# Moving 20 block dots in a hybrid GLA/DSA/PEER decoder kernel: between the gate blocks, a first weight tile fetched early, and a longer spread

## The chip, the cores and the metric

The kernel runs on one core of one Trainium2 chip. The metric is the device time of one launch in microseconds (us); a time in a table is the median of several runs. A profile is one execution of its own, recorded by the hardware profiler, with its own time.

## What is computed

One decoder layer on 512 tokens with model width 1024: two token mixers (gated linear attention and an attention over keys that an indexer selects), merged by sigmoid gates, and then a channel mixer with product keys (PEER). The change lies in the last part, which is, cut to what matters:

```python
q = (h @ w_q).reshape(B, S, PEER_HEADS, PEER_DKEY)
s1, s2 = q[..., :half] @ sub_keys_1.T, q[..., half:] @ sub_keys_2.T
v1, i1 = lax.top_k(s1, 16); v2, i2 = lax.top_k(s2, 16)
best, ci = lax.top_k((v1[..., :, None] + v2[..., None, :]).reshape(B, S, 8, 256), 16)
expert_idx = i1[ci // 16] * 128 + i2[ci % 16]          # 16384 experts
gates = jax.nn.softmax(best, axis=-1)
# per token: 8 heads x 16 experts
u, v = expert_u[expert_idx], expert_v[expert_idx]      # rows of 1024
a = gelu(einsum('td,thkd->thk', h, u)) * gates
out = einsum('thk,thkd->td', a, v)
x = rmsnorm(x + gate2 * out)
```

Everything is float32.

## The kernel before

Tokens come in four tiles of 128. The first two tiles are computed sparsely: GpSimd gathers for each token its expert rows by indirect DMAs (`fetch`), VectorE does the dot products and the weighted sums (`dot`, `add`, in the profile `grow`, `gacc`, `h2n`). This runs as a background generator `gather`, which `pump` moves on a step at a time between the steps of the other work.

The last two tiles (256 tokens) are computed densely, against all 16384 experts in 128 blocks of 128. For each block three things are needed:

- the **dot** (`dots_of(ib)`): the block's rows of `u` (`up`, one 1 MiB load for two blocks) times the 256 tokens, 8 float32 matmuls of 128x256, each of which the trace records as two passes, so 16 rows of `pmm<-h2h,up` on line 184. ScalarE puts the gelu into `kept[:, ib % 48]` (or, for tokens whose gates are there already, into `dg`, and VectorE multiplies `kept` by `dg`, line 956);
- the **gates** of the block: `build_g(Tt)` makes them for 8 tokens a step, 16 steps for a token tile. VectorE makes one-hot matrices `pm` and `eq` (lines 883, 886), ScalarE scales `eq` to `qm`, TensorE multiplies the two for each token (`products`, line 907, 8 matmuls a step, 16 passes), ScalarE copies the product to `gs`; every second step VectorE multiplies the `m` blocks of `kept` that have their dots by the new gates, ScalarE copies the gates of the others up to block 48, and the gates of blocks 48 to 127 go to DRAM (`gd<-gs`);
- the **chunk** `ib` of `dense`: the weights of the block (`kept`, split into a high and a low part `as`) times the block's rows of `v` (`vb`, split into `vs`), 12 matmuls of 128x512 that add into four PSUM banks (`psc`, `ptr`; lines 186 to 188).

The dots of blocks 0 to 47 (`AHEAD`) are made before `dense` starts; `DOTS = (8, 16)` says how many stand in the code ahead of the selection (`pick`) of the first and of the second dense token tile, and the rest follow in a loop with the gate steps of the second tile. While `pick` of the second tile runs, the loop takes two steps of the first tile's gates after each of its parts. The dots of blocks 48 to 127 are spread over the chunks: after chunk `ib`, dots are made up to number 48 + (ib + 1) * 80 // 112. The block's gates are read back as `gtile` (eight blocks in 1 MiB) and multiplied in by `weigh(ib + LEAD)`.

Engines run their instructions in order, and the order is that of a scheduler which moves instructions ahead where tiles allow it, so that the order of the code is only a preference. The tiles of `dense` lie in a pool `dn`, opened after the pool of the routing and of the gates (`rest_eng`) is closed; its addresses become free when that pool's work has ended. Two tiles of the pool `hp`, tags `hh` and `hl`, hold `up` loads of the early dots (the pairs of blocks rotate over two slots `w2`, `hh` and `hl`, so blocks 44 and 45 are in `hh`, 46 and 47 in `hl`), and afterwards `as4` (tag `hh`) and every second `gtile` (tag `hl`). All loads but the gathers stand in one queue, SP's.

Of the kernel before, what the change touches and what calls it, by code (L numbers as in the profile page):

```python
# [9 lines left out]
F32 = mybir.dt.float32  # L10
F32R = mybir.dt.float32r
# [9 lines left out]
P = 128  # L21
T = 512
D = 1024
# [16 lines left out]
NE = 7  # L40
RATE_ADA, RATE_GLA, RATE_DSA, RATE_G, RATE_DENSE = 0.4, 0.75, 0.9, 1.0, 1.05
AHEAD = 48
LEAD = 5
DOTS = (8, 16)
RATE_SEL = 3.0
GB = 16
HG = 4
# [2 lines left out]
NDT = T - TH  # L50
# [9 lines left out]
def hybrid_block_kernel(ctx, tc, x, c_col, w_ada, b_ada, b_col, g1_col, g2_col, wT, wN, wM, w_br, w_o,  # L60
                        w_gu, gla_g, kv_g, w_ukv, w_pq, sk, rows, u_t, v_t, fin_g, out):
    nc = tc.nc
    sb = ctx.enter_context(tc.tile_pool(name="const", bufs=1))
    dr = ctx.enter_context(tc.tile_pool(name="dr", bufs=1, space=DRAM))
    hp = ctx.enter_context(tc.tile_pool(name="acts", bufs=1))
# [45 lines left out]
    def behind(i):  # L111

        pace[0] = i.ins
# [10 lines left out]
    def pmm(narrow=False):  # L124
        turn[2] += 1
        if turn[2] % 3 == 0 and not narrow:
            return pmx()
        return ps.tile([P, 512], F32, name="pmm", bufs=2)
# [16 lines left out]
    def pump(n=1.0):  # L145

        if quiet[0]:
            return
        for b in background:
            b[2] += n * b[1]  # L150
            while b[2] >= 1:
                b[2] -= 1
                next(b[0], None)
# [36 lines left out]
    def projT(dst, src, act):  # L190

        w = [t.rearrange("p (k c) -> p k c", k=KD) for t in (src if isinstance(src, list) else weights(src, D, len(act) == 1))]
        for k in range(KD):
            mm(dst, [t[:, k] for t in w], [t[:, k] for t in act], k == 0, k == KD - 1)
# [18 lines left out]
    def drain(gen):  # L213
        for _ in gen:
            pass
# [660 lines left out]
    def build_g(Tt):  # L876

        TB = 8
        gs = None
        last = ()  # L880
        for t0 in range((Tt - NG) * P, (Tt - NG + 1) * P, TB):
            pm = gb.tile([P, TB, P], F32, name="pm", bufs=2)
            nc.vector.tensor_tensor(pm, iof[:, None, :].to_broadcast([P, TB, P]),
                                    i2T[:, t0:t0 + TB, None].to_broadcast([P, TB, P]), op=ALU.is_equal)
            e = gb.tile([P, TB // 2, P, 2], BF16, name="eq", bufs=2)
            behind(nc.vector.tensor_tensor(
                e, iob[:, None].to_broadcast([P, TB // 2, P, 2]),
                i1T[:, t0:t0 + TB].rearrange("p (g t) -> p g t", t=2)[:, :, None, :].to_broadcast([P, TB // 2, P, 2]),
                op=ALU.is_equal))
            qm = gb.tile([P, TB, P], F32, name="qm", bufs=2)  # L890
            for t in range(TB):
                nc.scalar.activation(qm[:, t], e[:, t // 2, :, t % 2], AF.Copy, scale=gaT[:, t0 + t:t0 + t + 1])
            drain(last)
            if t0 % GB == 0:
                gs = gb.tile([P, P, GB], F32, name="gs", bufs=2)
            last = products(t0, pm, qm, gs)
            pump()
            yield
        drain(last)

    def products(t0, pm, qm, gs):
        b, tb = t0 % GB, t0 // GB
        for t4_ in range(0, 8, 4):
            turn[0] += 1
            p = (psc, ptr)[turn[0] % 2]().rearrange("p (t i) -> p t i", t=4)
            for t in range(4):
                nc.tensor.matmul(p[:, t], pm[:, t4_ + t], qm[:, t4_ + t], start=True, stop=True)
            nc.scalar.copy(gs[:, :, b + t4_:b + t4_ + 4], p.rearrange("p t i -> p i t"))
        if b:

            m, ts_ = made[0], slice(tb * GB, (tb + 1) * GB)
            if m:
                nc.vector.tensor_tensor(kept[:, :m, ts_], kept[:, :m, ts_], gs[:, :m], op=ALU.mult)
            if m < AHEAD:
                nc.scalar.copy(kept[:, m:, ts_], gs[:, m:AHEAD])
            built[0] = (tb + 1) * GB
            nc.sync.dma_start(gd.rearrange("c p b i t -> b p c i t")[tb], gs.rearrange("p (c i) t -> p c i t", i=8)[:, AHEAD // 8:])
        yield
# [16 lines left out]
            nc.vector.scalar_tensor_tensor(y[:, ns], x2[:, ns], r, fing[:, ns], op0=ALU.mult, op1=ALU.mult)  # L935
            nc.sync.dma_start(out[Tt * P:(Tt + 1) * P, ns], y[:, ns])

    up = [None]

    def dots_of(ib):  # L940

        early = dn is None
        if ib % 2 == 0:
            pool, tag, bufs = ((wp, "w2", 2), (wp, "w2", 2), (hp, "hh", 1), (hp, "hl", 1))[ib // 2 % 4] if early else (dn, "up", 2)
            up[0] = pool.tile([P, 2, D], F32, name="up", tag=tag, bufs=bufs)
            nc.sync.dma_start(up[0], u_t[ib // 2])
        p = pmm(True)
        projT(p[:, :NDT], [up[0][:, ib % 2]], h2[1])
        a = kept[:, ib % AHEAD]
        d = built[0] if ib < AHEAD else 0  # L950
        if d < NDT:
            nc.scalar.activation(a[:, d:], p[:, d:NDT], AF.Gelu)
        if d:
            t = gb.tile([P, NDT], F32, name="dg", bufs=2)[:, :d]
            nc.scalar.activation(t, p[:, :d], AF.Gelu)
            behind(nc.vector.tensor_tensor(a[:, :d], a[:, :d], t, op=ALU.mult))
        made[0] += 1

    def dense(first_v):
        banks = [psc, psc, ptr, ptr]  # L960
        acc = [[banks[2 * i + n]() for n in range(2)] for i in range(NT - NG)]
        as4 = hp.tile([P, 4, 2, NDT], F32R, name="as", tag="hh")
        gts = []

        def load_g(c):

            if c < P // 8:
                pool, tag = ((dn, "gtile"), (hp, "hl"))[c % 2]
                gts.append(pool.tile([P, NDT // GB, 8, GB], F32, name="gtile", tag=tag))
                nc.sync.dma_start(gts[-1], gd[c - AHEAD // 8])  # L970

        load_g(AHEAD // 8)

        def weigh(ib):

            if ib < AHEAD:
                return
            if ib % 8 == 0:
                load_g(ib // 8 + 1)
            a3 = kept[:, ib % AHEAD].rearrange("p (b t) -> p b t", t=GB)  # L980
            behind(nc.vector.tensor_tensor(a3, a3, gts[ib // 8 - AHEAD // 8][:, :, ib % 8], op=ALU.mult))

        late_ops = []
        vb = x2 = None
        for ib in range(P):
            if ib < NRAW:
                vc = first_v[ib]
            elif ib % 2 == 0 or ib == NRAW:
                vb = dn.tile([P, 2, D], F32, name="vb", bufs=3)
                nc.sync.dma_start(vb[:, ib % 2:], v_t[ib // 2][:, ib % 2:])  # L990
            if ib >= NRAW:
                vc = vb[:, ib % 2]
            if ib == P - 8:
                x2 = dn.tile([P, NT - NG, D], F32, name="fx", tag="up", bufs=2)
                for i in range(NT - NG):
                    nc.sync.dma_start(x2[:, i], x2d[NG + i])
            if ib + LEAD < P:
                weigh(ib + LEAD)
            a = as4[:, ib % 4]
            v = wp.tile([P, 2, D], F32R, name="vs", tag="w2", bufs=2)  # L1000
            split(a[:, 0], a[:, 1], kept[:, ib % AHEAD])
            split(v[:, 0], v[:, 1], vc)
            a, v = [[t[:, 0], t[:, 1]] for t in (a, v)]
            late_ops.append((ib, a, v))
            stage[0] = ib
            if ib == P - 2:
                continue
            for i in range(NT - NG):
                ts_ = slice(i * P, (i + 1) * P)
                for n in range(2):  # L1010
                    ns = slice(n * 512, (n + 1) * 512)
                    for jb, a, v in late_ops:
                        mm(acc[i][n], [t[:, ts_] for t in a], [t[:, ns] for t in v], jb == 0, jb == P - 1)
            late_ops.clear()
            while made[0] < AHEAD + (ib + 1) * (P - AHEAD) // (P - 16) and made[0] < P:
                dots_of(made[0])
            pump()
        for i in range(NT - NG):
            finish(NG + i, x2[:, i], acc[i])
# [90 lines left out]
    dn = None  # L1110
# [47 lines left out]
    made, built = [0], [0]  # L1158
    building = iter(())
    background[:] = [[gat, RATE_G, 0.0]]  # L1160
    for Tt in range(NG, NT):
        for _ in range(DOTS[Tt - NG]):
            dots_of(made[0])
        for h0 in range(0, 8, HG):
            for _ in pick(Tt, h0):
                next(building, None)
                next(building, None)
                pump(0.6)
        picks_T(Tt)
        drain(building)  # L1170
        building = build_g(Tt)
# [6 lines left out]
    for ib in range(NRAW):  # L1178
        first_v.append(wp.tile([P, D], F32, name="vc", tag="raw", bufs=NRAW))
        nc.sync.dma_start(first_v[ib], v_t[ib // 2][:, ib % 2])  # L1180
    rest_eng.close()
    dn = ctx.enter_context(tc.tile_pool(name="dn", bufs=1, reuse_waits="tile"))
    fing, gate2 = [dn.tile([P, D], F32, name=n) for n in ("fing", "gate2")]
# [72 lines left out]
```

## Time and profile before

| | us |
|---|---|
| median of 3 runs | 1851.52 (1850.68 to 1851.56) |
| the profiled execution | 1843.28 |
| its span, first to last instruction | 1841.6 |
| TensorE (PE) busy in the span | 1717.2 |
| VectorE (DVE) busy | 1430.3 |
| ScalarE (ACT) busy | 718.8 |
| GpSimd (POOL) busy | 555.5 |

The span is the stretch from the first to the last instruction of the profiled execution; its time has 1.7 us around it. An engine's busy time is the sum of its instructions. PE's instructions are pipelined, so that a duration covers the next one's start: the pitch of two starts is what one of them costs when PE is full. The stages meant in this document lie in the span at these places: the dots, the second `pick` and the gates from 957.6 to 1178.2 us, the chunks from 1178.2 to 1829.5, the last normalization from there to 1841.6.

### The profile page before, as it was taken

The numbers are of one execution on the slowest core, as the hardware profiler recorded it, in microseconds if no ns is written. First come the engines' busy times: TensorE is split into PE (matmuls) and PEld (weight loads), VectorE is DVE, ScalarE is ACT, GpSimd is POOL, SyncE is SP. The second block draws the span as 40 slices with busy tenths as digits, with TensorE's granted clock in tenths as the row PEclk, the third lists the DMA queues.
The fourth block names the chain that finished last, engine by engine and source line by source line (L and its number), as shares of the span: only waits on it lengthen the run. The fifth ranks groups of instructions, "written<-read, shape, count | busy, mean of one in ns | idle before, by whom it ended". The sixth has DMA issues, their size and how long they took to land.

```text
span 1841.6 us, 25048 instructions
## 1 busy us (share of the span) xinstructions
PE 1717.2 (93%) x8898; PEld 1461.0 (79%) x8898; DVE 1430.3 (78%) x2985; ACT 718.8 (39%) x1694; POOL 555.5 (30%) x459
## 2 busy tenths in 40 slices
PE   6999999989999988988999889899999999999995
PEld 3887999978767776877778779788888888888874
DVE  5698646438999868766996999388888888788887
ACT  3544465432221124102243878334333333333343
POOL 0013000001454456652432667122222222222220
PEclk9999999989998999989999889999999999999998
DMA  7747556724887799996876999799999999999992
GB/s 289 278 166 281 197 172 212 252 86 178 282 305 250 267 353 375 389 378 239 321 285 248 339 324 382 302 395 407 407 415 398 400 398 414 393 406 405 400 351 116
DMA packets 145567, 573.33 MB, mean 311 GB/s; under 512 B 14481, under 2 KB 41233, under 8 KB 111650
## 3 DMA queue, kind: packets, MB, share of 16 engines
q1 hardware_dynamic: 90146, 303.28, 44.4%
q0 software_dynamic: 55296, 268.46, 37.6%
q8 instruction: 70, 1.15, 0.2%
q14 instruction: 55, 0.45, 0.1%
HBM read 553.86 MB, written 17.83 MB: 310 GB/s over the span
## 4 chain that ended last, share of the span: by engine, by line
PE 40%; issue 22%; DVE 19%; DMA 8%; POOL 8%; ACT 2%; POOLq 0%; SPq 0%; DVEq 0%; ACTq 0%
PE pmm L184 14%; POOL grow L1022 7%; DMA grow<-rows,ids 7%; DVE gacc L1036 3%; DVE grow L1027 3%; PE pmm L187 2%; PE pmm L188 2%; PE pmm L186 2%; PE pmx L184 2%; PE psc L187 1%; PE psc L188 1%; PE psc L186 1%; PE ptr L187 1%; PE ptr L186 1%; PE ptr L188 1%
## 5 line engine op out<-in xcount | busy, mean ns | idle before, releaser
L1022 POOL DMA_INDIRECT grow<-rows,ids x384 | 496.5, 1293 | 842.9 <-DVE h2n L1036 461.1
L184 PE MATMUL pmm<-h2h,up 128*128 128x256 f32 x2048 | 470.7, 383 | 13.4 <-DMA up<-u_t 6.7
L184 PEld LDWEIGHTS pmm<-h2h,up 128*128 128x128 f32 x2048 | 388.3, 192 | 69.6 <-DMA up<-u_t 7.1
L1027 DVE SCALAR_TENSOR_TENSOR grow<-grow,h2n 128x1024 f32<-128x1024 f32 x256 | 310.8, 1220 | 68.3 <-DMA grow<-rows,ids 68.0
L117 DVE TENSOR_TENSOR vs<-vb,vs 128x1024 fp32r<-128x1024 f32 x125 | 152.9, 1223 | 40.5 <-ACT vs L116 40.2
L1036 DVE SCALAR_TENSOR_TENSOR gacc<-grow,dots,gacc 128x1024 f32<-128x1024 f32 x127 | 162.7, 1281 | 15.2 <-DMA grow<-rows,ids 14.8
L1036 DVE SCALAR_TENSOR_TENSOR h2n<-grow,dots,h2n 128x1024 f32<-128x1024 f32 x127 | 162.8, 1282 | 0.0
L116 ACT CAST vs<-vb 128x1024 fp32r<-128x1024 f32 x125 | 130.3, 1043 | 14.0 <-DMA vb<-v_t 10.1
L117 DVE TENSOR_TENSOR w<-raw,w 128x1024 fp32r<-128x1024 f32 x79 | 98.0, 1241 | 46.5 <-ACT w L116 46.2
L186 PE MATMUL psc<-vs,as 128*128 128x512 f32 x256 | 113.9, 451 | 0.0
L187 PE MATMUL psc<-vs,as 128*128 128x512 f32 x256 | 101.8, 398 | 11.2 <-DVE vs L117 11.1
L116 ACT CAST w<-raw 128x1024 fp32r<-128x1024 f32 x79 | 82.7, 1046 | 74.2 <-PE pmm L188 35.6
L1075 ACT ACTIVATE dots<-dots 128x1 f32<-128x1 f32 x128 | 25.8, 202 | 199.1 <-DVE grow L1027 199.0
L116 ACT CAST as<-kept 128x256 fp32r<-128x256 f32 x128 | 51.3, 403 | 128.2 <-PE ptr L187 128.2
L184 PE MATMUL pmm<-hh,raw 128*128 128x256 f32 x416 | 97.6, 382 | 3.6 <-DVE yp L687 1.8
L188 PE MATMUL psc<-vs,as 128*128 128x512 f32 x256 | 100.5, 393 | 0.0
L187 PE MATMUL ptr<-vs,as 128*128 128x512 f32 x256 | 100.1, 391 | 0.0
L188 PE MATMUL ptr<-vs,as 128*128 128x512 f32 x256 | 100.1, 391 | 0.0
L186 PE MATMUL ptr<-vs,as 128*128 128x512 f32 x256 | 98.8, 391 | 0.0
L94 POOL TENSOR_TENSOR rs<-rs,mhalf 128x1 f32<-128x1 f32 (+1 forms) x24 | 18.1, 754 | 265.8 <-DVE rs L93 265.7
L184 PEld LDWEIGHTS pmm<-hh,raw 128*128 128x128 f32 x416 | 76.5, 190 | 16.0 <-DVE yp L687 2.2
L117 DVE TENSOR_TENSOR as<-kept,as 128x256 fp32r<-128x256 f32 x128 | 53.4, 424 | 45.5 <-ACT as L116 45.5
(379 smaller groups left out, 3527.6 us busy)
## 6 DMA issues: line engine op xcount, KB each, us to landing
up<-u_t SPq DMA_DIRECT2D x64, 1024.0 KB, 9.4
vb<-v_t SPq DMA_DIRECT2D x62, 1024.0 KB, 8.9
raw<-wT SPq DMA_DIRECT2D x74, 512.0 KB, 4.9
adaw<-w_ada SPq DMA_DIRECT2D x20, 1024.0 KB, 7.8
raw<-wN SPq DMA_DIRECT2D x32, 512.0 KB, 4.5
raw<-w_br SPq DMA_DIRECT2D x32, 512.0 KB, 4.6
raw<-w_pq SPq DMA_DIRECT2D x32, 512.0 KB, 4.5
gd<-gs SPq DMA_DIRECT2D x16, 640.0 KB, 8.2
```

Source lines behind the costliest of these rows:

```text
L94: nc.gpsimd.tensor_tensor(dst, dst, mhalf[:, :w], op=ALU.pow)
L116: (hi_eng or nc.scalar.copy)(hi, src)
L117: i = (eng or nc.vector).tensor_tensor(lo, src, hi.bitcast(F32), op=ALU.subtract)
L184: nc.tensor.matmul(dst, a[0], b[0], start=first, stop=last, **kw)
L186: nc.tensor.matmul(dst, a[0], b[0], start=first, stop=False, **kw)
L187: nc.tensor.matmul(dst, a[0], b[1], start=False, stop=False, **kw)
L188: nc.tensor.matmul(dst, a[1], b[0], start=False, stop=last, **kw)
L1022: nc.gpsimd.indirect_dma_start(out=dst, out_offset=None, in_=table, in_offset=bass.IndirectOffsetOnAxis(ap=index[0][:, r:r + 1], axis=0))
L1027: nc.vector.scalar_tensor_tensor(u, u, 1.0, h2n[i], op0=ALU.mult, op1=ALU.mult, accum_out=dots[i][:, r:r + 1])
L1036: nc.vector.scalar_tensor_tensor(gacc, v, w, gacc, op0=ALU.mult, op1=ALU.add)
L1075: nc.scalar.activation(w, w, AF.Gelu)
```

## The change

1. `DOTS` goes from (8, 16) to (8, 4), and `build_g` now yields `True` after each of its steps: in the loop over the second `pick`, each step of the first tile's gates is followed by one dot. So 12 dots less stand ahead of the second `pick`, 16 are made between the steps of the first tile's gates, and 20 instead of 24 are left for the loop over the second tile's gates.
2. The `up` tile of blocks 48 and 49 is loaded into tag `hh` of the pool `hp` before `dn` is opened, and `dots_of(48)` takes it. `as4` moves to tag `hl`, and the `gtile` that lay in `hl` moves to `hh`.
3. The 80 dots in `dense` are spread over 122 chunks instead of 112 (`P - LEAD - 3` for `P - 16`), and `LEAD` is 3 instead of 5.

```diff
-LEAD = 5
-DOTS = (8, 16)
+LEAD = 3
+DOTS = (8, 4)
...
             last = products(t0, pm, qm, gs)
             pump()
-            yield
+            yield True
...
-    up = [None]
+    up, next_up = [None], []
...
-        if ib % 2 == 0:
+        if ib == AHEAD:
+            up[0] = next_up[0]
+        elif ib % 2 == 0:
...
-        as4 = hp.tile([P, 4, 2, NDT], F32R, name="as", tag="hh")
+        as4 = hp.tile([P, 4, 2, NDT], F32R, name="as", tag="hl")
...
-                pool, tag = ((dn, "gtile"), (hp, "hl"))[c % 2]
+                pool, tag = ((dn, "gtile"), (hp, "hh"))[c % 2]
...
-            while made[0] < AHEAD + (ib + 1) * (P - AHEAD) // (P - 16) and made[0] < P:
+            while made[0] < AHEAD + (ib + 1) * (P - AHEAD) // (P - LEAD - 3) and made[0] < P:
                 dots_of(made[0])
...
             for _ in pick(Tt, h0):
-                next(building, None)
-                next(building, None)
+                for _ in range(2):
+                    if next(building, None):
+                        dots_of(made[0])
                 pump(0.6)
...
         nc.sync.dma_start(first_v[ib], v_t[ib // 2][:, ib % 2])
+
+    next_up.append(hp.tile([P, 2, D], F32, name="up", tag="hh"))
+    nc.sync.dma_start(next_up[0], u_t[AHEAD // 2])
     rest_eng.close()
```

On TensorE the order of instructions is the same up to the transposition of the first dense tile's picks (line 873). The rows from there to the third gate step, where `L184 ... pmm<-h2h,up` are dots (8 instructions each) and `L907` the products of a gate step, with - what stood there and + what stands there now:

```order
 L873 MATMUL psc<-ident,mi 128x128
-L184 MATMUL pmm<-h2h,up 128x256 x105
+L184 MATMUL pmm<-h2h,up 128x256 x17
 L907 MATMUL psc<-qm,pm 128x128 x4
 L907 MATMUL ptr<-qm,pm 128x128 x4
+L184 MATMUL pmm<-h2h,up 128x256 x8
 L907 MATMUL psc<-qm,pm 128x128 x4
 L907 MATMUL ptr<-qm,pm 128x128 x4
+L184 MATMUL pmm<-h2h,up 128x256 x8
 L907 MATMUL psc<-qm,pm 128x128 x4
 L907 MATMUL ptr<-qm,pm 128x128 x4
```

Eleven dots that stood ahead of the first gate products now stand behind them, one between two gate steps.

SP's queue where `dense` begins, before (`vb` are rows of `v`, `fing` and `gate_9544` two vectors for the end):

```order
L917 DMA gd<-gs 128x10x128
L1086 DMA fx<-x2d_90 128x1024
L970 DMA gtile<-gd 128x2048
L1184 DMA fing<-fin_g 128x1024
L1185 DMA gate_9544<-gated_104 128x1024
L970 DMA gtile<-gd 128x2048
L946 DMA up<-u_t 128x2048
L990 DMA vb<-v_t 128x1024
```

and of the change:

```order
L1088 DMA fx<-x2d_90 128x1024
L917 DMA gd<-gs 128x10x128
L1186 DMA up<-u_t 128x2048
L1190 DMA fing<-fin_g 128x1024
L1191 DMA gate_9580<-gated_104 128x1024
L972 DMA gtile<-gd 128x2048
L992 DMA vb<-v_t 128x1024
```

The `up` load of blocks 48 and 49 moves from behind four loads to the place right behind the last store of gates, and one of the two `gtile` loads ahead of the first `vb` is gone from there (it comes later, in `hh`). On TensorE the last dots ahead of the first chunk are now 26 instructions, three dots and the first two matmuls of block 48's, where 56, seven dots, stood.

The end of SP's queue, before:

```order
L946 DMA up<-u_t 128x2048
L990 DMA vb<-v_t 128x2048 x2
L996 DMA fx<-x2d_92 128x1024
L996 DMA fx<-x2d_93 128x1024
L990 DMA vb<-v_t 128x2048 x5
L936 DMA out_dram<-fy 128x512 x6
```

and of the change:

```order
L948 DMA up<-u_t 128x2048
L992 DMA vb<-v_t 128x2048 x2
L998 DMA fx<-x2d_92 128x1024
L998 DMA fx<-x2d_93 128x1024
L992 DMA vb<-v_t 128x2048
L948 DMA up<-u_t 128x2048
L992 DMA vb<-v_t 128x2048
L936 DMA out_dram<-fy 128x512 x6
```

The last pair of dots is loaded five `vb` loads (ten chunks) later with respect to the chunks. On TensorE the last dot now has 6 chunks behind it.

## Rows read from the trace of the kernel before

**Rows 1.** The page: span, busy us of each engine (share, instructions).

```profile
span 1841.6 us, 25048 instructions
...
PE 1717.2 (93%) x8898; PEld 1461.0 (79%) x8898; DVE 1430.3 (78%) x2985; ACT 718.8 (39%) x1694; POOL 555.5 (30%) x459
```

**Rows 2.** Busy us of PE, PEld, DVE, ACT, POOL; clock, DMA share, GB/s.

```profile
957.60:1155.90 198.30, 180.26 (x1009) 162.84 (x1008) 175.16 (x270) 137.38 (x399) 110.19 (x69) 0.92 0.89 318
...
1005.80:1081.60 75.80, 59.97 (x335) 54.21 (x334) 70.60 (x73) 58.76 (x171) 46.73 (x33) 0.80 0.90 318
1081.60:1154.20 72.60, 72.60 (x455) 66.98 (x454) 68.73 (x82) 60.05 (x187) 50.97 (x27) 1.00 1.01 364
...
1178.20:1829.50 651.30, 633.38 (x2817) 533.71 (x2816) 529.63 (x727) 250.69 (x590) 157.30 (x124) 0.99 0.95 384
...
1200.00:1777.00 577.00, 576.89 (x2601) 490.53 (x2600) 477.66 (x658) 224.35 (x538) 146.86 (x117) 1.00 0.99 402
...
1829.50:1841.60 12.10, 0.45 (x2) 0.02 (x1) 6.04 (x13) 2.61 (x8) 1.41 (x2) 0.65 0.23 87
```

**Rows 3.** PE's timeline, 958 to 1178 us: start, length, instructions, [idle before, releaser].

```profile
958.01 21.32 PE L184 MATMUL pmm<-h2h,up 128*128 128x256 f32 x98
981.54 24.44 PE L184 MATMUL pmm<-h2h,up 128*128 128x256 f32 x112 [2.21 <-ACT kept L952]
...
1040.01 1.43 PE L907 MATMUL psc<-qm,pm 128*128 128x128 f32 x8 [2.77 <-ACT qm L892]
...
1153.33 1.06 PE L907 MATMUL ptr<-qm,pm 128*128 128x128 f32 x8
1154.23 24.34 PE L184 MATMUL pmm<-h2h,up 128*128 128x256 f32 x112
```

**Rows 4.** The same windows view for tile pmm (two stretches) and line 907 (one).

```profile
957.60:1178.20 220.60, 139.22 (x597) 110.40 (x595) 0.00 (x0) 15.71 (x54) 0.93 0.86 309
...
1200.00:1777.00 577.00, 284.84 (x1262) 238.79 (x1260) 0.00 (x0) 29.53 (x79) 1.00 0.99 402
...
957.60:1178.20 220.60, 78.38 (x512) 75.35 (x512) 0.93 0.86 309
```

**Rows 5.** Groups by line, DVE, 957.6 to 1155.9 us: busy, mean ns | idle before.

```profile
L883 DVE TENSOR_TENSOR pm<-iof,i2T 128x1024 f32<-128x1024 bf16 x32 | 39.2, 1225 | 11.9 <-PE ptr L907 11.9
...
L956 DVE TENSOR_TENSOR kept<-kept,dg 128x128 f32<-128x128 f32 x3 | 0.9, 289 | 0.0
```

**Rows 6.** PE's waits from 1178 us to the end: us in total, times, longest.

```profile
PE psc L187 <- DVE vs L117: 11.1, 7, 7.0
PE pmm L184 <- DMA up<-u_t: 6.7, 1, 6.7
```

**Rows 7.** PE's timeline at the first chunks (12 instructions a chunk).

```profile
1178.21 0.58 PE L186 MATMUL psc<-vs,as 128*128 128x512 f32 x1
...
1181.17 0.39 PE L186 MATMUL psc<-vs,as 128*128 128x512 f32 x1
...
1183.89 0.39 PE L186 MATMUL psc<-vs,as 128*128 128x512 f32 x1
...
1193.44 6.91 PE L184 MATMUL pmm<-h2h,up 128*128 128x256 f32 x20 [6.67 <-DMA up<-u_t]
```

**Rows 8.** SP's queue in the timeline around 1180 us.

```profile
1178.60 0.33 SPq L970 DMA_DIRECT2D gtile<-gd  x1
...
1180.74 0.43 SPq L946 DMA_DIRECT2D up<-u_t  x1
```

**Rows 9.** DMA from 1200 to 1777 us; an issue's last number: us to landing.

```profile
DMA packets 32229, 231.78 MB, mean 402 GB/s; under 512 B 3574, under 2 KB 3574, under 8 KB 4214
...
up<-u_t SPq DMA_DIRECT2D x38, 1024.0 KB, 10.2
```

**Rows 10.** Two of the 20 us windows of the chunks, columns as in Rows 2.

```profile
1210.00:1230.00 20.00, 20.00 (x92) 17.00 (x91) 15.52 (x22) 6.76 (x18) 4.79 (x4) 1.00 1.01 424
...
1590.00:1610.00 20.00, 20.00 (x91) 16.94 (x91) 14.86 (x22) 8.61 (x20) 7.16 (x5) 1.00 0.92 365
```

## The prediction

> **What bounds the kernel now.** I read first the page: TensorE is busy for 1717 of 1841.6 us, 93% [rows 1]. A share like that says only that PE is near the limit on the whole, so the second view is the table of stretches [rows 2]. From 1200 to 1777 us, the chunks with dots between them, PE is busy for 576.9 of 577 us at a granted clock of 1.00: nothing but work of PE counts there. In two other places it is different. From 1005.8 to 1081.6 us, the first tile's gates, PE is busy for 60.0 of 75.8 us and at a clock of 0.80, that is partly on the lower of its two levels, while VectorE is busy for 70.6. And over all chunks, 1178.2 to 1829.5, PE's 633.4 busy us include time at half clock. So what the change can win lies where PE stands or runs slowly, not in the 577 us.
>
> Third, PE's own timeline tells why it stands [rows 3]. From 958.0 on, 210 passes of dots (13 dots) run in one piece until 1005.8, and only then the first gate products come. VectorE has by then both `pm` buffers full and waits 11.9 us for these products [rows 5]. Afterwards VectorE is the slow one: PE waits 2.77 us for `qm` at 1040, and more such waits follow. From 1154.2 to 1178.2 seven dots run alone, with little for VectorE to do. PE work and VectorE work follow one another here, where they could overlap.
>
> Fourth, PE's waits in `dense` [rows 6]: 6.7 us once for the first `up` tile, 11.1 us in seven waits for VectorE's `vs`. These seven lie in the last 15 chunks, which have no dots between them, so that PE asks for a chunk faster than VectorE, with the last gathers still to add, can split one.
>
> **Prices.** A dot is 16 passes; 112 of them start at 1154.23 and the next instruction at 1178.21 [rows 3, 7], so a pass costs 0.2141 us and a dot 3.43. A chunk's 12 matmuls cost 1183.89 - 1181.17 = 2.72 us [rows 7]. Eight passes of gate products cost 1154.23 - 1153.33 = 0.90 [rows 3].
>
> **Part 1, dots between the gate steps.** From 957.6 to 1178.2 PE has 597 passes of dots and 512 of gate products [rows 4]: 127.8 + 57.6 = 185.4 us at full clock, of 220.6. VectorE has 175.2 us of work until 1155.9 [rows 2]. The change leaves both sums nearly as they are, but the first gate products come 11 dots, 37.7 us, earlier in PE's order, and a dot follows each gate step. It adds work: 16 dots now meet gates that exist already, so each has one more multiplication of `kept` by `dg` on VectorE, over 16 to 128 columns. At 128 columns one costs 0.289 us [rows 5], so 16 cost at most 4.6; for columns that grow evenly I take 3.5. The extra gelu piece on ScalarE (137.4 of 198.3 us busy [rows 2]) lies under other work; if it did not, it would be another 4 us or so, by VectorE's figure. No DMA is added; eleven dots' `up` loads move some tens of us later.
>
> Then VectorE is the longer one. It ends the gates at 957.6 + 175.2 + 3.5 + its idle time. That was 198.3 - 175.2 = 23.1 us, of which 11.9 was the wait for the late products. I take this wait as gone and the other 11.2 as staying: 1147.5. PE's last gate product ended 1.7 us before VectorE's end (1154.2 against 1155.9), so its last dots begin at 1145.8; now there are three in place of seven, 10.3 us: 1156.1 in place of 1178.2, **22.1 us won**. Bounds: with no idle time at all, 33 us; with PE, ScalarE and VectorE waiting for each other a second 17 us, 5. I take the middle because from 1081.6 to 1154.2, with dots and gate steps alternating in the old order too, PE was busy for 72.6 of 72.6 us and VectorE for 68.7 [rows 2].
>
> **Part 2, the first `up` tile.** In the old queue `up` was issued at 1180.74, right after a `gtile` load that had held SP until 1178.60, the end of block 47's dot [rows 8]; PE then waited 6.67 us, and its next 20 passes took 6.91 us in place of 4.28, on the lower clock [rows 7]: 9.3 us lost. Now the load waits for `hh`, that is for block 45's dot, two dots (6.9 us) before PE wants it, and needs 10.2 us to land [rows 9]: a wait of 3.3 us is left. Its first two matmuls stand ahead of chunk 0 in PE's order, so all chunks queue behind that wait. `as4` in `hl` now needs block 47's dot to end before it can be written; the nearest wait of that kind in the rows is PE's 2.21 us for a gelu [rows 3], and I count nothing for it since the 3.3 us cover it. If they do not, it is up to 2.2. The `gtile` in `hh` is wanted nine blocks later and costs nothing in that cover. The same holds for `LEAD`: even the last dot now ends six chunks, 16 us, before its chunk, while a weighing is one multiplication over 256 columns, of the kind that takes 0.289 us over 128 [rows 5].
>
> **Part 3, 122 chunks.** PE's work in `dense` does not change: 128 x 2.72 + 80 x 3.43 = 622.6 us of the 651.3 [rows 2]. What changes is where it lies. Up to chunk 121 a chunk now costs PE 2.72 + 80/122 x 3.43 = 4.97 us (5.17 measured: 577 us with 1262 passes of dots and 1339 other matmuls, 111.6 chunks [rows 2, 4]), and only 6 chunks are bare. VectorE had 477.7 us for those 111.6 chunks, 4.28 each, so it keeps up with 4.97.
>
> What it takes from DMA is the question. It moved 231.78 MB in that stretch [rows 9], 2.077 MB a chunk, at 402 GB/s and a share of 0.99. Now it is 0.05 dots of 0.524 MB less, 2.050 MB, and at 4.97 us a chunk that asks for 412 GB/s. In full windows the engines reached 424 at a share of 1.01; in windows with the short pieces of `gtile`, 365 [rows 10]. Scaled, the share would be 0.99 x (2.050 / 2.077) x (5.17 / 4.97) = 1.017, just over that ceiling, so DMA's own pace is about 5.00 us a chunk and there is no slack for a late transfer. I take 5.05: 122 x 5.05 + 6 x 2.72 + 3.3 = 635.7 in place of 651.3, **15.6 us won**. Bounds: 25 with PE alone (4.97), nothing at 5.18.
>
> On the same question the Trainium skill (DMA: Bandwidth & Descriptors, Specifications) gives 435 GB/s as the fabric's ceiling and about 358 GB/s as the share of HBM that one core gets. The trace does not agree that 358 binds here: 402 was held for 577 us. By 435 a chunk would need 4.71 us and PE would stay the bound.
>
> **The sum.** 22.1 + 15.6 = 37.7. The profiled execution took 1843.3, so 1805.6. The runs had a median of 1851.5, 8.2 above it; the same difference on both sides gives **1814**.
>
> **The rivals.**
> - *A: DMA takes back what part 3 gives.* Already at 0.99 of its share, it paces the chunks at 5.18 or so: 1851.5 - 22 = 1830. For it: the share and VectorE's waits between gathers; against it: PE had no wait at 402 GB/s. 15%.
> - *B: the gate steps run in lockstep.* Each dot needs ScalarE's gelu to free its bank, each product needs `qm`, and PE takes them strictly in turn, at a lower clock if it pauses, as it did at 0.80. Then some 5 us of part 1 remain: 1851.5 - 5 - 15.6 = 1831. Against it stands the stretch to 1154.2. 14%.
> - *C: slower.* The same transfers in less time are more than DMA can do, and all chunks run at the rate of the worse windows, 365 GB/s: 2.050 MB take 5.62 us, 122 x 5.62 + 19.6 = 705, 54 us more, less part 1: 1883. It decides from a chunk of 5.36 us on (651.3 + 22.1 = 673.4; less 19.6, over 122), 382 GB/s. Against it: full windows did 424. 8%. By the 358 GB/s of the Trainium skill it would be 1896.
> - *D: nothing to be seen.* A and B both, and B's last 5 us gone to the added multiplications of VectorE (4.6 at most): 1851. 5%.
>
> **How the numbers follow.** My forecast has 58%, and its own range is 1803 to 1827 (48 to 25 won). To leave out no more than 2 in 10 the range must take in A and B: 1801 to 1838. What can be told from no change in this kernel is 0.2%, 3.7 us. Faster by more than that are the forecast, A and B: 87%; D gives 5% for the same, C 8% for slower.
>
> **What would show it.** Right: first gate products near 970 in place of 1005.8, the clock at 1.00 through the gates, the first chunk near 1156 to 1160, a wait for `up` under 4 us, a chunk of 5.0 to 5.1 us, no waits for `vs` at the end, DMA's share above 1.00. Wrong: many PE waits for `qm` or `dg` among the gates, a first chunk after 1170, PE waits for `up`, `vb` or `vs` in the middle of the chunks.

## The result and the profile after

| us | before | after |
|---|---|---|
| median of the runs compared | 1851.1 (4 runs, 1841.74 to 1851.56) | 1803.15 (4 runs, 1801.99 to 1806.42) |
| the profiled execution | 1843.28 | 1806.42 |
| its span | 1841.6 | 1804.7 |

The ratio is 0.9756, with a 95% interval of 0.9722 to 0.9789: 45 us faster (39 to 51). In a later set of runs it was 0.9743 (0.9718 to 0.9768).

The page of the changed kernel, which answers to [rows 1]:

```profile
span 1804.7 us, 25065 instructions
...
PE 1709.3 (95%) x8898; PEld 1455.6 (81%) x8898; DVE 1429.5 (79%) x2995; ACT 717.9 (40%) x1708; POOL 548.8 (30%) x459
```

The engines' work is the same as before to within 1.2%; the span is 36.9 us shorter. So work was moved under other work, and none was saved. Where, the table of stretches shows (columns as in [rows 2]): the gates from the transposed picks of line 873 to VectorE's last piece of them, the chunks, and the full middle of the chunks.

```profile
964.40:1147.80 183.40, 181.03 (x1074) 164.36 (x1073) 181.45 (x292) 140.98 (x422) 111.01 (x72) 1.00 0.97 354
...
1160.80:1793.10 632.30, 630.03 (x2814) 532.30 (x2812) 530.92 (x727) 249.92 (x590) 152.43 (x124) 0.99 0.96 392
1200.00:1740.00 540.00, 539.57 (x2427) 457.35 (x2426) 463.33 (x634) 215.77 (x517) 140.38 (x114) 1.00 1.00 412
```

In the gates both PE (181.0 of 183.4 us) and VectorE (181.5) are now busy all the time, at a granted clock of 1.00; before, it was 180.3 and 175.2 of 198.3 us at 0.92 [rows 2]. PE's timeline, to be read beside [rows 3, 7]:

```profile
964.27 0.27 PE L873 MATMUL psc<-ident,mi 128*128 128x128 f32 x1
964.38 7.50 PE L184 MATMUL pmm<-h2h,up 128*128 128x256 f32 x34
971.72 1.05 PE L907 MATMUL psc<-qm,pm 128*128 128x128 f32 x8
972.61 1.06 PE L907 MATMUL ptr<-qm,pm 128*128 128x128 f32 x8
973.51 3.62 PE L184 MATMUL pmm<-h2h,up 128*128 128x256 f32 x16
...
1145.46 10.53 PE L184 MATMUL pmm<-h2h,up 128*128 128x256 f32 x48
1160.05 1.10 PE L184 MATMUL pmm<-h2h,up 128*128 128x256 f32 x4 [4.06 <-DMA up<-u_t]
1160.80 0.59 PE L186 MATMUL psc<-vs,as 128*128 128x512 f32 x1
...
1165.34 0.40 PE L186 MATMUL psc<-vs,as 128*128 128x512 f32 x1
```

Somewhat over two dots (34 passes), a gate step, one dot, a gate step: the order that the change wrote. The first gate products come 7.5 us after the picks, where it was 47.9. Behind the gates only three dots are left (48 passes), then PE waits 4.06 us for the first `up` tile, makes the first two matmuls of block 48's dot (4 passes), and chunk 0 begins. With line 873 as the mark, which stood at 957.90 before, the span divides so:

- up to line 873: 6.4 us longer. PE's order of instructions is the same up to there. Over the fourteen profiles of this study the mark lies between 956.5 and 966.6, and a second profile of the changed kernel has it at 959.6: much of this is the spread of single executions. But the three kernels without part 2 of the change have the mark at 956.5 to 957.9, and the eleven profiles with it at 959.3 or later, so that some of it may belong to part 2; no run here separates the two.
- from there to the end of the last dots ahead of the chunks: 1155.99 - 964.27 = 191.7 where it was 220.3, 28.6 us less.
- from there to the start of the last chunk's last matmul (1792.74; before 1829.56): 636.8 where it was 651.4, 14.6 us less, the wait for `up` included.
- the tail: 12.0 us both times.

PE's waits from 957.6 us to the end (columns as in [rows 6]):

```profile
PE pmm L184 <- DMA up<-u_t: 5.9, 2, 4.1
...
PE psc L907 <- ACT qm L892: 1.5, 1, 1.5
...
PE psc L187 <- DVE vs L117: 0.4, 1, 0.4
```

The seven waits for `vs` at the end, 11.1 us, are gone but for 0.4. In the middle, dots and DMA from 1200 to 1740 us (columns as in [rows 4, 9]):

```profile
1200.00:1740.00 540.00, 255.29 (x1131) 213.99 (x1130) 0.00 (x0) 26.60 (x71) 1.00 1.00 412
```

```profile
DMA packets 30784, 222.22 MB, mean 412 GB/s; under 512 B 3422, under 2 KB 3422, under 8 KB 3806
```

2427 - 1131 = 1296 matmuls of chunks, 108 chunks in 540 us: 5.00 us each, 2.058 MB each, and PE stands for 0.4 us in all.

### The profile page after: what moved, and what is told of

Read it like the earlier page. It is cut to its first block, busy times and chain, and to the rows that moved or that the text cites. A ratio compares the mean times of both kernels' runs of the same rounds, so it can differ in the third digit from the quotient of the medians.

```text
span 1804.7 us, 25065 instructions
## 1 busy us (share of the span) xinstructions
PE 1709.3 (95%) x8898; PEld 1455.6 (81%) x8898; DVE 1429.5 (79%) x2995; ACT 717.9 (40%) x1708; POOL 548.8 (30%) x459
## 4 chain that ended last, share of the span: by engine, by line
PE 29%; issue 29%; DVE 19%; POOL 11%; DMA 8%; ACT 2%; SPq 0%; POOLq 0%; DVEq 0%; another core or an unknown queue 0%; ACTq 0%
POOL grow L1024 10%; PE pmm L184 8%; DMA grow<-rows,ids 6%; DVE gacc L1038 4%; DVE grow L1029 3%; PE pmx L184 2%; PE pmm L188 2%; PE pmm L187 2%; PE pmm L186 2%; DMA adaw<-w_ada 1%; DVE pm L883 1%; PE pmx L187 1%; PE pmx L186 1%; PE pmx L188 1%; DVE score L489 1%
## 5 line engine op out<-in xcount | busy, mean ns | idle before, releaser
L1024 POOL DMA_INDIRECT grow<-rows,ids x384 | 491.0, 1279 | 807.2 <-DVE h2n L1038 441.6
L184 PE MATMUL pmm<-h2h,up 128*128 128x256 f32 x2048 | 467.7, 381 | 7.7 <-DMA up<-u_t 6.8
L184 PEld LDWEIGHTS pmm<-h2h,up 128*128 128x128 f32 x2048 | 386.5, 191 | 63.5 <-issue 4.6
L1029 DVE SCALAR_TENSOR_TENSOR grow<-grow,h2n 128x1024 f32<-128x1024 f32 x256 | 310.9, 1220 | 95.4 <-DMA grow<-rows,ids 93.1
L184 PE MATMUL pmm<-hh,raw 128*128 128x256 f32 x416 | 99.7, 388 | 5.0 <-DVE bsg L689 2.5
L184 PEld LDWEIGHTS pmm<-hh,raw 128*128 128x128 f32 x416 | 77.9, 194 | 18.2 <-DVE bsg L689 3.3
L892 ACT ACTIVATE qm<-eq,gaT 128x128 f32<-128x128 bf16 x256 | 79.0, 390 | 18.5 <-DVE eq L886 17.1
```

The lines of the kernel that those rows point to most:

```text
L184: nc.tensor.matmul(dst, a[0], b[0], start=first, stop=last, **kw)
L1024: nc.gpsimd.indirect_dma_start(out=dst, out_offset=None, in_=table, in_offset=bass.IndirectOffsetOnAxis(ap=index[0][:, r:r + 1], axis=0))
L1029: nc.vector.scalar_tensor_tensor(u, u, 1.0, h2n[i], op0=ALU.mult, op1=ALU.mult, accum_out=dots[i][:, r:r + 1])
```

## The experiments

### Each part alone, and two of them together

Part 1 alone (`p1_gates`), the kernel before with

```diff
-DOTS = (8, 16)
+DOTS = (8, 4)
...
-            yield
+            yield True
...
-                next(building, None)
-                next(building, None)
+                for _ in range(2):
+                    if next(building, None):
+                        dots_of(made[0])
```

> Only part 1: 12 dots less ahead of the second selection and one dot behind each gate step of the first tile; the first up tile and the spread over 112 chunks as before. Theory (the three parts add up, each where it was read): in the profile of the change the stretch from the transposed picks to the end of the last dot ahead of the chunks was shorter by 28 us, and the rest stays, with PE's 6.7 us wait for up and the 11 us of waits for vs at the end: 25 to 29 us less than before, ratio 0.984 to 0.987. Rival (the early gates only move the load on DMA, the chunks then start with a longer backlog): less than 15 us, ratio above 0.992.

Part 2 alone (`p2_up`):

```diff
+        if ib == AHEAD:
+            up[0] = next_up[0]
...
+    next_up.append(hp.tile([P, 2, D], F32, name="up", tag="hh"))
+    nc.sync.dma_start(next_up[0], u_t[AHEAD // 2])
```

with `as4` and the odd `gtile` exchanged between `hl` and `hh`.

> Only part 2: the up tile of blocks 48 and 49 loaded ahead into hh, as4 in hl, the second gtile in hh. Theory: PE's wait of 6.7 us and the 2.6 us at half clock behind it go; a wait of 3 to 4 us comes, with some half clock of its own: 3 to 6 us less, ratio 0.997 to 0.998. Rival (the load only takes the place of other loads, and the next wait, for vb, comes instead): no difference, 0.999 to 1.001.

Part 3 alone (`p3_spread`):

```diff
-LEAD = 5
+LEAD = 3
...
-            while made[0] < AHEAD + (ib + 1) * (P - AHEAD) // (P - 16) and made[0] < P:
+            while made[0] < AHEAD + (ib + 1) * (P - AHEAD) // (P - LEAD - 3) and made[0] < P:
```

> Only part 3: 122 chunks in place of 112, LEAD 3 in place of 5. Theory: 12 to 16 us less, since the waits for vs at the end go and DMA can just supply a chunk of 5.00 us; chunks of 5.00 us in the profile, ratio 0.991 to 0.994. Rival A of the prediction (DMA paces the chunks at about 5.18): no difference, ratio 0.999 to 1.001.

The changed kernel without part 3 (`a_112`):

```diff
-LEAD = 3
+LEAD = 5
...
-            while made[0] < AHEAD + (ib + 1) * (P - AHEAD) // (P - LEAD - 3) and made[0] < P:
+            while made[0] < AHEAD + (ib + 1) * (P - AHEAD) // (P - 16) and made[0] < P:
```

> Parts 1 and 2 without part 3: the changed kernel with 112 chunks and LEAD 5. Theory (the parts add up): 28 to 35 us less than before, ratio 0.981 to 0.985, so 12 to 16 us more than the changed kernel. Rival (the spread gives nothing): as the changed kernel, 0.974 to 0.977.

The four ran beside the kernel before (1841.17):

| | time | ratio (95% interval) | line 873 to first chunk | first chunk to last matmul |
|---|---|---|---|---|
| before | 1841.17 | | 220.3 | 651.4 |
| p1_gates | 1816.3 | 0.9867 (0.9841 to 0.9893) | 191.6 | 653.0 |
| p2_up | 1837.3 | 0.9976 (0.9960 to 0.9991) | 222.2 | 639.8 |
| p3_spread | 1829.45 | 0.9946 (0.9923 to 0.9969) | 218.9 | 637.6 |
| a_112 | 1807.96 | 0.9815 (0.9793 to 0.9838) | 196.5 | 643.2 |
| the change | 1803.15 | 0.9756 (0.9722 to 0.9789) | 196.5 | 631.9 |

(The two columns on the right are of single profiles; for before and the change they are those of the first section, and so are the change's time and ratio, from a set of its own.) By the ratios the parts win 1.33%, 0.24% and 0.54%, 24.5, 4.4 and 10 us; their sum, 2.11%, is beside the 2.44% (2.1 to 2.8) of the whole. Part 1's gain lies ahead of the first chunk and is not given back behind it; parts 2 and 3 win in the chunks. Part 1 and part 3 came out below what was expected of them: 24.5 us where 25 to 29 were, and 10 (5.7 to 14) where 12 to 16 were. Part 2 won the 3 to 6 expected; its profile is 9.7 us shorter behind line 873, but the line itself stands 8.7 us later in it. PE's waits in `p1_gates` and in `a_112` show what the parts left out would have taken away:

```profile
PE pmm L184 <- DMA up<-u_t: 10.3, 1, 10.3
PE psc L187 <- DVE vs L117: 9.0, 7, 4.2
```

```profile
PE psc L187 <- DVE vs L117: 9.8, 7, 4.0
PE pmm L184 <- DMA up<-u_t: 3.7, 2, 3.2
```

With part 1 alone the dots are done sooner and the wait for the first `up` tile grows from 6.7 [rows 6] to 10.3 us; part 2 cuts it to between 2.6 and 4.1 us (2.57 in `p2_up`, 3.15 in `a_112`, 4.06 and 2.81 in the two profiles of the change). The seven waits for `vs` stay until the dots reach nearly to the last chunk.

### What part 1 needs: an early first step, or the alternation

The changed kernel without the dots between the gate steps (`a_noyield`):

```diff
-            yield True
+            yield
```

> The changed kernel without the dots between the gate steps of the first tile: DOTS stays (8, 4), but the 16 dots are made later, in the loop over the second tile's gates and behind it. Theory (the gain of part 1 needs both, gates that start earlier and dots that fill PE while VectorE makes them): the gates start as early as in the changed kernel, PE then stands and falls to its lower clock for the rest of the first tile, and some 16 dots, 55 us, run alone at the end: 30 to 45 us slower than the changed kernel, ratio to before 0.993 to 1.003. Rival (the earlier start of the gates is enough, since PE has slack): as the changed kernel, 0.974 to 0.980.

Measured: 1852.26, ratio to before 1.0045 (1.0029 to 1.0060); beside the change's 0.9756 that is 53 us slower than the change, where the theory said 30 to 45. Twelve dots fewer ahead of the gates with none between them is a little slower than the kernel before. The same 100 us of `a_noyield`, then of the change (columns as in [rows 2]):

```profile
970.00:1070.00 100.00, 64.24 (x337) 58.49 (x337) 100.00 (x185) 69.65 (x188) 62.16 (x44) 0.81 0.91 301
```

```profile
970.00:1070.00 100.00, 97.63 (x565) 87.52 (x564) 100.00 (x197) 73.02 (x210) 64.47 (x43) 1.00 1.00 363
```

VectorE is busy for all of it in both, so it sets the pace of the gates; without dots between them PE is busy for 64.2 us at a granted clock of 0.81, and the dots that would have filled the other 36 come later: the first chunk starts 246.2 us after line 873, not 196.5.

The changed kernel with the dots of the table back (`a_dots16`), so that the alternation stays but begins later:

```diff
-DOTS = (8, 4)
+DOTS = (8, 16)
```

> The changed kernel with the table of dots back at 16, so that twelve dots more stand ahead of the first gate products (some 40 us of dots in one piece again), while a dot still follows each gate step of the first tile. Theory (the gain of part 1 comes from starting the gate products early, since VectorE's own 180 us of work then set the end): most of part 1 is lost, the first gate products come some 45 us after the transposed picks, the first chunk some 215 us after them in place of 196.5, and the time is 12 to 22 us above the changed kernel in the same call. Rival (what counts is that dots and gate steps alternate, wherever the first products stand): the same as the changed kernel within 4 us.

Measured: 1838.47, ratio 0.9956 (0.9935 to 0.9977), 37 us above the change in the same set (1801.06). PE's timeline and three stretches:

```profile
966.56 21.32 PE L184 MATMUL pmm<-h2h,up 128*128 128x256 f32 x98
990.39 27.89 PE L184 MATMUL pmm<-h2h,up 128*128 128x256 f32 x128 [2.52 <-ACT kept L954]
1018.12 1.05 PE L907 MATMUL psc<-qm,pm 128*128 128x128 f32 x8
...
1185.54 0.79 PE L186 MATMUL psc<-vs,as 128*128 128x512 f32 x1 [2.11 <-ACT as L116]
...
1207.84 1.22 PE L186 MATMUL psc<-vs,as 128*128 128x512 f32 x2 [11.26 <-ACT vs L116]
```

```profile
966.50:1017.50 51.00, 48.48 (x226) 42.37 (x225) 34.49 (x115) 17.84 (x39) 12.60 (x10) 1.00 0.65 236
1017.50:1163.00 145.50, 140.13 (x845) 128.93 (x844) 127.71 (x144) 106.04 (x324) 86.04 (x54) 0.96 0.92 322
1163.00:1185.60 22.60, 13.84 (x78) 12.42 (x76) 19.99 (x23) 16.20 (x48) 8.74 (x7) 0.82 0.86 275
```

Now VectorE has 34.5 us of work in the first 51 us, and at the end of the gates PE has none to fill its pauses (13.8 of 22.6 busy). The first chunk starts 219.1 us after line 873, as the theory said, and 20 us later than in the change's profile of the same set (198.8). So both halves of part 1 count: the dots must lie under VectorE's gates from the first step to the last. A cost that neither theory had came on top. No dots are left behind the gates, and in SP's queue the loads for the chunks stand behind a `gtile` that waits until the last gates have landed in DRAM:

```profile
SPq L972 <- DMA gd<-gs: 2.0, 1, 2.0
```

```profile
1188.95 0.32 SPq L972 DMA_DIRECT2D gtile<-gd  x1
1189.33 0.97 SPq L992 DMA_DIRECT2D vb<-v_t  x2
```

That is 3.4 us after chunk 0 has begun; in the change `gtile` waits for the same thing, but under the last dots, and is issued at 1157.56, 3.2 us ahead of chunk 0. After three chunks PE runs out of `vs`, which ScalarE can't split before `vb` lands, and waits 11.26 us. From the first chunk to the last matmul it took 647.4 us, 13.3 more than the change in this set. With the 20 us that is some 34 us, of the 37 between the medians; the theory's 12 to 22 had only the first. (Both profiles are the slowest run of their kernel in the set.)

### Has DMA anything left at 412 GB/s?

A load of 0.131 MB that nothing uses, written into the code of each of the chunks 4 to 121 (`a_moredma`), and the same with half the bytes and three times the buffers (`a_moredma6`; its lines are shown):

```diff
+            if NRAW < ib < P - 6:
+                more = dn.tile([P, 128], F32, name="more_", bufs=6)
+                nc.sync.dma_start(more, v_t[ib // 2][:, 0, :128])
             if ib == P - 8:
```

> The changed kernel with one more load of 0.131 MB a chunk in SP's queue, into a tile that nobody reads, for chunks 4 to 121. Theory (DMA has no slack left at a share of 1.00: the full windows moved 424 GB/s, and a chunk of 2.058 + 0.131 MB at that rate takes 5.16 us in place of 5.00): 15 to 25 us slower than the changed kernel, PE waiting for up, vb or vs in the middle of the chunks, ratio to before 0.983 to 0.990. Rival (a share of 1.00 is not yet the ceiling): chunks stay at 5.00 us, less than 4 us slower, 0.974 to 0.978.

Measured: 1916.34, ratio 1.0389 (1.0373 to 1.0405); beside the change's 0.9756 that is some 117 us above it, far more than either said. SP's waits show why this run says little of DMA. With two buffers, loads stood in SP's queue until the one two loads before had landed, and all loads behind them stood too; the longest of these waits:

```profile
SPq L997 <- DMA more__11625<-v_t: 15.5, 1, 15.5
```

From 1220 to 1740 us DMA moved only 354 GB/s at a share of 0.91; over the whole run from 957.6 us on PE waited 88.4 us for `up`. Nor did the loads go out one a chunk: the scheduler moved them ahead of their places, and SP issued the last at 1556.9 us, so that none was left for the rest of the chunks.

> The changed kernel with 0.066 MB more to load in each of chunks 4 to 121 (data that nothing uses, into six buffers in turn, so that SP's queue should seldom stand for them): 2.124 MB a chunk in place of 2.058. Theory (DMA has no slack left at 412 GB/s, the changed kernel's pace): a chunk of 5.15 us, 12 to 20 us more than the changed kernel, with PE waits for up or vs in the chunks. Rival (PE still sets the pace, DMA goes on to the 424 GB/s of full windows): a chunk of 5.01 us, 0 to 4 us more.

Measured: 1842.58, ratio 0.9996 (0.9975 to 1.0017), 41.5 us above the change in the same set. Here too the loads were moved ahead; SP issued all 118 between 1155.9 and 1379.0 us, in the time of some 39 chunks. The last of them:

```profile
1378.98 0.43 SPq L997 DMA_DIRECT2D more__13746<-v_t  x1
```

So the chunks have a stretch with these loads and one without. All of PE's work in the two, and then its dots alone (columns as in [rows 2, 4]):

```profile
1220.00:1420.00 200.00, 170.10 (x716) 141.03 (x715) 137.78 (x188) 64.11 (x152) 42.41 (x34) 0.91 0.97 376
1420.00:1740.00 320.00, 319.76 (x1441) 271.48 (x1440) 272.86 (x372) 127.43 (x305) 81.59 (x67) 1.00 1.00 410
```

```profile
1220.00:1420.00 200.00, 82.83 (x332) 67.65 (x331) 0.00 (x0) 7.95 (x21) 0.91 0.97 376
1420.00:1740.00 320.00, 151.57 (x673) 127.17 (x672) 0.00 (x0) 15.73 (x42) 1.00 1.00 410
```

With the loads, (716 - 332) / 12 = 32 chunks took 200 us, 6.25 us each; without them, (1441 - 673) / 12 = 64 took 320 us, 5.00 each as in the change. Thirty-two chunks at 1.25 us more are 40 us, the whole of the loss. Theory and rival both counted on one load a chunk, 3% more bytes; what ran was three loads a chunk for a third of the way and then none. So neither is decided: whether DMA has room for 3% more bytes, up to the 424 GB/s of full windows, stays open.

What a small load costs DMA can be estimated. DMA over the 520 us from 1220 us in `a_moredma6`, and its hardware queue (packets, MB, share of 16 engines):

```profile
DMA packets 41538, 206.47 MB, mean 397 GB/s; under 512 B 4609, under 2 KB 16863, under 8 KB 17247
q1 hardware_dynamic: 26988, 100.31, 48.8%
```

and the same queue in the change:

```profile
q1 hardware_dynamic: 13958, 99.60, 46.7%
```

The packets from 512 B to 2 KB are those of the small loads, 128 for each: (16863 - 4609) / 128 = 96 loads (95.7), 6.3 MB. In the change the queue took 46.7% of 520 us for 99.60 MB, 2.44 us a MB; at that rate the other 94.0 MB of `a_moredma6` account for 44.1%, and the 96 small loads for the remaining 4.7%, 0.256 us each, where their bytes alone would be 0.160. (The Trainium skill, DMA: Bandwidth & Descriptors, Bandwidth, says that transfers under 64 KB are dominated by their descriptors and gives 138 GB/s for a transfer of 64 KB from GpSimd's queue; here it is, by the estimate, 0.0655 MB in 0.256 us, 256 GB/s, beside loads in flight: less than the 410 GB/s of the queue's large loads, so the direction agrees.) 118 such loads are 30 us of the 41.5. The other 11 I can't divide: PE's lower clock after its waits (0.91 from 1220 to 1420), and SP's queue, which stood up to 8.0 us for some of these loads.

### Smaller questions

`LEAD` alone (`a_lead5`, the 122 chunks kept):

```diff
-LEAD = 3
+LEAD = 5
...
-            while made[0] < AHEAD + (ib + 1) * (P - AHEAD) // (P - LEAD - 3) and made[0] < P:
+            while made[0] < AHEAD + (ib + 1) * (P - AHEAD) // (P - 6) and made[0] < P:
```

> The changed kernel with LEAD 5 in place of 3, the spread still over 122 chunks. Theory (the weighing is placed by its dot, LEAD costs and gives nothing): as the changed kernel, ratio to before 0.974 to 0.978. Rival (an earlier place of the weighing makes VectorE wait for dots that are not there near the end, where the last dots are five or six chunks ahead): 3 us or more slower than the changed kernel, 0.979 or above.

Measured: 1805.6, ratio 0.9779 (0.9756 to 0.9803). How far ahead a block is weighed can't be seen in the time.

Tile `hh` free two dots earlier, to take away the 4.06 us wait, first by itself (`a_rot`) and then beside the change (`a_rot_again`, `after_again`):

```diff
-            pool, tag, bufs = ((wp, "w2", 2), (wp, "w2", 2), (hp, "hh", 1), (hp, "hl", 1))[ib // 2 % 4] if early else (dn, "up", 2)
+            pool, tag, bufs = ((wp, "w2", 2), (wp, "w2", 2), (hp, "hh", 1), (hp, "hl", 1))[(ib // 2 + 1) % 4] if early else (dn, "up", 2)
```

> The changed kernel with the pairs of early blocks rotated by one over the four tiles, so that blocks 42 and 43 lie in hh and the load of blocks 48 and 49 can start two dots earlier; blocks 46 and 47 then lie in a slot that the second chunk's vs needs. Theory (the wait for that load, 4.1 us and 1.8 us of half clock in the profile of the change, is only a matter of when hh comes free): 3 to 6 us less than the changed kernel, ratio to before 0.971 to 0.975, no wait of PE for up ahead of chunk 0, under 1.5 us for vs at chunk 1. Rival (the load is late because DMA is full at the end of the gates, so an earlier issue only delays the gathers): as the changed kernel, 0.974 to 0.978.

> The changed kernel again, against the kernel before, as the comparison for the others of this call: a ratio of 0.972 to 0.982, as before.

> The rotation of the early pairs by one again (tile hh free two dots earlier, so that the first up tile of the chunks lands in time), now beside the changed kernel itself. Theory (the 4 us wait for up at the first chunk is still lost time): 2 to 4 us less than the changed kernel. Rival (it comes back as waits elsewhere, as the first look showed): the same within 2 us.

Measured: `a_rot` 1803.87, ratio 0.9774 (0.9753 to 0.9796); then `a_rot_again` 1801.57, 0.9768 (0.9744 to 0.9792), beside the change at 1801.06, 0.9743 (0.9718 to 0.9768). The wait ahead of chunk 0 is gone in its profile, and in its place PE waits for later `up` tiles:

```profile
PE pmm L184 <- DMA up<-u_t: 6.1, 3, 3.9
```

No gain can be measured, as the rival said: `a_rot_again` and the change can't be told apart.

## Why the prediction was right, and where its sizes were off

**What it is.** 1803.15 lies in the range of 1801 to 1838 and at the fast end of the forecast's own, 1803 to 1827. The mechanism was the forecast's; the rivals didn't happen.

**Part 1** was mis-sized: 22.1 us predicted, 28.6 in the two profiles, 28.7 in the profile of part 1 alone (220.3 to 191.6). By the times of part 1 alone it is 24.5 (20 to 29), so the miss is seen in the profiles and not in the times. The step that failed is "the other 11.2 as staying": I kept all of VectorE's idle time but the wait for the late products. Of the gates' 183.4 us VectorE was idle for 2.0, so 9.2 of those 11.2 went too; its work grew by 6.3 us (175.16 to 181.45) and not by 3.5, which leaves 6.5. VectorE's waits of the kernel before (957.6 to 1180 us, columns as in [rows 6]; most of those for `dg` lie behind the gates, 1.8 us in them) show what I had kept:

```profile
DVE kept L956 <- ACT dg L955: 13.6, 6, 3.0
DVE pm L883 <- PE ptr L907: 11.9, 2, 11.3
DVE gacc L1036 <- DMA grow<-rows,ids: 4.5, 3, 3.4
DVE kept L913 <- ACT gs L908: 4.5, 3, 2.1
DVE eq L886 <- ACT i1T L872: 0.7, 1, 0.7
```

Behind the 11.9 us for the late products stand 7.0 for ScalarE and 4.5 for gathered rows. In the change's gates they are 1.2 and 1.5, in those of part 1 alone 1.5 and 0.9; without part 1 they stay, 5.4 and 4.4 in `p3_spread`. So most of them went with part 1 here; by which way, for the gathered rows above all, no run shows. (Nor do they go in every profile: in the gates of `a_rot`, which has part 1, ScalarE's are 9.7.) Of the 6.3, the added multiplications are 2.7, of which this is the group of the change, then of before (columns as in [rows 5]):

```profile
L958 DVE TENSOR_TENSOR kept<-kept,dg 128x128 f32<-128x128 f32 (+14 forms) x31 | 8.6, 281 | 0.0
```

```profile
L956 DVE TENSOR_TENSOR kept<-kept,dg 128x128 f32<-128x128 f32 (+7 forms) x17 | 5.9, 349 | 1.8 <-ACT dg L955 1.8
```

The other 3.6 are work of VectorE that fell into this stretch, of the last gathers and the first `vs`. Had rival B, the lockstep, held, PE would have waited for `qm` again and again between the dots; in the change it did so once, for 1.5 us. (In `a_noyield`, without these dots, it did 12 times, 33.2 us in all.)

**Part 2.** A wait of 3.3 us was left in the sum; 4.06 was measured. The clock behind it was put at nothing in the sum, without a reason: the granted clock was 0.65 from 1160.05 to 1164.51, partly the lower of the two levels, so that chunk 0 took 4.54 us (1160.80 to 1165.34) in place of 2.72. By itself the part won 4.4 us (1.7 to 7.4), and 9.3 - 3.3 = 6.0 had been predicted.

**Part 3.** 122 chunks at 5.05 us were predicted, 5.00 were measured, DMA's pace as worked out (5.00) and 0.03 above PE's. Since PE was busy throughout, at a DMA share of 1.00, the two can't be told apart there. That is 6 us less; the longer wait (0.8), the slower chunk 0 (1.8) and a second wait for `up`, 1.84 us ahead of 1764.94 with 16 slow passes behind it (5.41 us in place of 3.43), gave it back, 6.4 us in all. Parts 2 and 3 together: 15.6 predicted, 14.6 measured. Rival A, 5.18 us a chunk, and rival C, 382 GB/s or less, fall by PE's 539.57 busy us of 540 at 412 GB/s. How near A was stays open: `a_moredma6` shows only that 118 small loads, three a chunk while they last, take back the whole gain of the change.

**The sum.** For the profiled execution 1805.6 was predicted and 1806.42 measured. That they agree to 0.8 us is luck, since two errors cancel there: part 1 won 6.5 us more, and this execution came 6.4 us later to line 873. "The same difference on both sides gives 1814" was the second step that failed: the profiled execution before was 8.2 us below the median, that after was the slowest of its four, 3.3 above. In ratios, 1805.6 / 1843.3 = 0.9795 is 7 us above the measured 0.9756, about the 6.5 us of part 1.

**What would show it.** The signs held: first gate products at 971.7, the clock at 1.00, a chunk of 5.00 us, and of the seven waits for `vs` one of 0.4 us is left. DMA's share was 1.00 over the stretch, where the sign said above 1.00, and 1.02 in a full window, at 421 GB/s. The wait for `up` was 0.06 us above the bound named, and the first chunk at 1160.8 just behind its place.

## What to carry to other kernels

When two engines that need each other are both nearly full in a stage, look at where their work lies before counting it: what stands at its start or its end for one engine alone is time in which the other does nothing. In such a stage don't keep the small waits when the large one goes: here most of them went with it, though they were for other things. Before the time of a probe is read, look at where its instructions ran: the loads written one a chunk ran three a chunk, and the run answered another question. And a profile is one execution of a spread: carry a predicted difference to the median as a ratio, and don't carry over how far the profiled run lay from it.

## What was not expected of the hardware

- DMA held 412 GB/s for 540 us, and 421 GB/s in windows of 20 us:

```profile
1700.00:1720.00 20.00, 20.00 (x92) 17.01 (x91) 16.62 (x23) 8.93 (x20) 4.18 (x4) 1.00 1.02 421
```

  The Trainium skill (HBM Reference, Specifications (TRN2)) says that a core which streams alone reaches about 425 GB/s, far above its 358 GB/s share; the runs agree, and rival C's 358 had no place here.
- The price of a pause of PE was not the pause alone: after 4.06 us without work the clock was 0.65 for the next 4.46 us.
- Small loads into few buffers cost far more than their bytes: 118 loads of 0.131 MB with two buffers, 0.31 us each at 424 GB/s, cost about 0.99 us each (117 us in all), while SP's queue stood for their buffers up to 15.5 us at a time. How much of it is the standing and how much the loads themselves, no run separates.
